# One seven-product step per unit turned into a mixed step, and another step's weight sum moved to the DMA, in a fused attention block

## The chip, the cores and the metric

The kernel runs on one core of a Trainium2 chip. The metric is the time on the device, in microseconds (us), of one execution; the median of three timed runs before the change is 1746.84 us (1742.09, 1746.84 and 1747.45). One further execution was recorded by the hardware profiler; it took 1742.72 us, and its span from the first to the last instruction is 1741.0 us.

## The reference

The input x has 256 rows of 4096 numbers. With the depth set to 1 only the attention layer runs:

```python
xn = rms_norm(x, norm_attn)
q, k, v, g = split(xn @ w_in_attn, 4)          # (256, 4096) @ (4096, 16384)
o = stick_breaking_attention(q, k, v)          # 32 heads of 128
h = x + (o * silu(g)) @ w_out_attn             # (256, 4096) @ (4096, 4096)
out = rms_norm(h, final_norm)
```

In the attention, each weight is a sigmoid of the scaled score times the product of one minus the sigmoids of the scores between it and the query, computed in log space, over strictly earlier positions.

Everything is float32. The two matrix products hold nearly all of the arithmetic.

## The kernel before, in words

**Exact products from three matmuls.** A float32 operand f is split into a rounded high part h (ScalarE casts it, `wh` for weights, `sh`/`oh` for the activations) and a low part l = f - h (VectorE subtracts, `wl`, `sl`/`ol`). A product is hh + hl + lh: three matmuls of 128x128 by 128x512 into one PSUM bank (`mm3`). So each weight tile costs one cast of ScalarE and one subtraction of VectorE before TensorE can use it.

**Units and steps.** The work is cut into 20 units. Units 0 to 15 belong to the input projection: unit u computes 256 columns of each of q, k, v and gate for all 256 rows. Units 16 to 19 belong to the output projection. A unit runs over the 4096 rows of its weights in 8 steps of 512 rows. A step has four raw weight tiles, named by (t, k): column half t, row half k, each 128x1024 numbers. They are loaded by SyncE into a ring of 8 buffers (`RAW_BUFS`), so two steps' tiles are held at a time; `load` (L427) issues them in a fixed order, and for steps with sums it takes the tile (1, 0) 2.5 places earlier.

**Saving products.** Units 0 and 16 are plain: 16 products per step. In all others a step seen as a 2x2 block product is of one of three kinds:

- a *full seven-product step* (`SEVEN_PARTS`, L97): a Strassen-like scheme. Seven weight parts, each of two 128x512 pieces, one product each: 14 products. Three of the seven parts are sums of raw tiles, beside a fourth that the load itself makes.
- an *eight-product step* (`EIGHT_PARTS`, L106): four parts, each used for two products per piece: 16 products, no sums of weights.
- a *mixed step* (`MIXED_PARTS`, L112): one of the two 128-row pieces goes by seven products, the other by eight: 15 products in six parts, the last with one piece only. Its sums are of 512 numbers per partition in place of 1024.

`SEVEN_IN` and `MIX_IN` list which steps of the input units are of the first and third kind, `SEVEN_AFTER` and `MIX_AFTER` those of the output units. Before, an input unit after the first has steps 1, 3, 4, 6 full, steps 0, 2, 5 mixed and step 7 eight-product: 4 x 14 + 3 x 15 + 16 = 117 products.

**The sums of weights.** For each full or mixed step:

- One sum (T3 in the code, `add_block`, L467) is made while loading: GpSimd issues a DMA that adds the block from memory onto the tile (1, 0): 512 KB for a full step, 256 KB for a mixed one.
- `sums` (L496) makes three more on VectorE: the difference for part 4, and the sums for parts 5 and 6 (for a mixed step: half as long, and the second of them is folded into part 4's tile).
- For the full steps listed in `FOURTH_IN` (input) the last sum, for part 6, is not made by VectorE but by a DMA that adds one SBUF buffer onto another (`moved_third`, L525), again issued by GpSimd, 512 KB. For these steps the difference is also due earlier (`FOURTH_AHEAD`, 6 us before its first product, against `SUMS_AHEAD`, 3 us).

Parts 5 and 6 of a step are used late: after the second part of the next step (L337 to L349). A step's tile is given back to the ring when its last subtraction and sum are done.

**Buffers.** There are 6 buffers for high parts (`PAIRS`) and 6 for low parts (`LOWS`), each of one part; ScalarE and VectorE can be at most six parts ahead of TensorE. The *lead* of a part is the time from the end of its low part on VectorE to its first matmul.

**The accumulators.** Seven PSUM banks hold the products of the scheme; at a unit's end `combine` (L805) adds them up on ScalarE and VectorE into `qk_sb` and `gv_sb`. The next unit's first products need those banks free. The eighth bank serves the attention of the two heads of the last unit (`head`, L929), whose small matmuls are put among the products of the following unit; its element work runs on ScalarE and VectorE.

**The order.** The class `Plan` (L139) runs a list schedule while the program is built: each engine has a clock, costs are formulas (`vector_ns`, `scalar_ns`, `tensor_ns`), and when an engine comes free the waiting operation with the earliest due time is emitted. Due times come from the place of a part's first product in the order of TensorE. The order of instructions on each engine is fixed by this; a change of the steps' kinds makes the whole order anew.

**The forms of x.** For each of 32 pieces of 128 rows of x (two per step) the forms for seven (7 forms) or eight products (6 forms) are made during unit 0 (`blocks_of`, `sums_of`); `SEVEN` (L88) has both pieces of a full step and the first of a mixed one.

The tables behind the counts above:

```python
SEVEN_PARTS = (
    part(0, 0, (1, "A11")), part(0, 1, (2, "A12")), part(1, 1, (3, "S4")),
    part(1, 0, (7, "S3")), part(0, 0, (6, "S2")), part(1, 1, (5, "S1")), part(0, 1, (4, "A22")),
)
MIXED_PARTS = (
    ((0, 0), 2, ((2, "A11", 1, 1), (4, "A21", 1, 1), (1, "A11", 0, 0))),
    ((0, 1), 2, ((2, "A12", 0, 0), (2, "A12", 1, 1), (4, "A22", 1, 1))),
    ((1, 1), 2, ((5, "A22", 1, 1), (3, "D2", 1, 1), (3, "S4", 0, 0))),
    ((1, 0), 2, ((5, "A21", 1, 1), (3, "D1", 1, 1), (7, "S3", 0, 0))),
    ((0, 0), 2, ((6, "S2", 0, 0), (4, "A22", 0, 1))),
    ((1, 1), 1, ((5, "S1", 0, 0),)),
)
```

Of the kernel before, what the change touches and what calls it, by code (L numbers as in the profile page):

```python
# [40 lines left out]

SEVEN_IN, MIX_IN = (1, 3, 4, 6), (0, 2, 5)
SEVEN_AFTER, MIX_AFTER = (1, 3, 6), (0, 2, 5)
RAW_BUFS = 8
PAIRS, LOWS = 6, 6
# [7 lines left out]
AHEAD, SUMS_AHEAD = 1.0, 3.0  # L55
PIPE = 1
T3_LEAD = 1500
FOURTH_IN, FOURTH_OUT = (1, 3), ()
FOURTH_AHEAD = 6.0
RAW_LEAD = 0  # L60
EARLY = 2.5
# [1382 lines left out]
```

## Time and profile before

| what | value |
|---|---|
| median of 3 timed runs | 1746.84 us |
| the profiled execution | 1742.72 us, span 1741.0 us |
| TensorE matmuls busy | 1713.9 us (98%) |
| TensorE weight loads busy | 1407.4 us (81%) |
| VectorE busy | 1630.2 us (94%) |
| ScalarE busy | 1227.0 us (70%) |
| GpSimd busy | 209.1 us (12%) |
| DMA | 434.84 MB, mean 250 GB/s |
| granted TensorE clock | 0.996 |

In the profile's rows PE is TensorE's matmuls, PEld its weight loads, DVE VectorE, ACT ScalarE, POOL GpSimd, and SP SyncE. A row of the order in time has the start in us from the span's start, the duration, the engine, the operation with out<-in, its shape, how many were merged (x), and in brackets the idle time before it and what ended it. A row of waits has who waited for whom, the total in us, how often, and the longest. All instructions show one line of the code (L158), since every one is issued through one helper of `Plan`, so rows are told apart by the names of tiles: `raw` raw weights, `wh` and `wl` their high and low parts, `acc` the PSUM banks, `sh`/`sl` forms of x, `oh`/`ol` forms of the attention's output.

### The profile page before, as it was taken

To read this page: it belongs to the slowest core of one execution; us is meant where nothing else is said; L and a number is where in the kernel's file an instruction comes from. 1 tells how busy PE (TensorE), PEld (TensorE's weight loads), DVE (VectorE), ACT (ScalarE), POOL (GpSimd) and SP (SyncE) were. 2 spreads that over 40 slices of the span, in tenths; PEclk is the share of its full clock that TensorE was granted. 3 is DMA by queue.
4 is the path that set the end of the run, shared out by engine and by line. 5 is a ranking of instruction groups with operands and counts; after the bars stand their busy time and mean duration, and the time that the engine had idled before them with its cause. 6 is when DMAs were issued, how large, how long until landed. Compare 5 with 4: busy or idle time off the path is not lost.

```text
span 1741.0 us, 23954 instructions
## 1 busy us (share of the span) xinstructions
PE 1713.9 (98%) x7690; PEld 1407.4 (81%) x7690; DVE 1630.2 (94%) x1872; ACT 1227.0 (70%) x1599; POOL 209.1 (12%) x224
## 2 busy tenths in 40 slices
PE   9999999999999999999999999999999999999997
PEld 6888888888888888888787878787888778888885
DVE  7889999999999999999999999999999987899997
ACT  7876777676777676767686767676767665666664
POOL 0010111011101011111111111111111022011100
PEclk9999999999999999999999999999999999999998
DMA  9998989888989898988888988889898778798886
GB/s 302 316 251 242 254 243 241 239 252 254 243 253 248 249 239 254 238 252 236 250 242 246 237 250 232 247 235 260 232 258 236 254 251 241 232 290 243 261 255 230
DMA packets 240543, 434.84 MB, mean 250 GB/s; under 512 B 25472, under 2 KB 45440, under 8 KB 240416
## 3 DMA queue, kind: packets, MB, share of 16 engines
q1 hardware_dynamic: 197616, 354.24, 62.0%
q0 software_dynamic: 41504, 77.22, 24.4%
q10 hardware_dynamic: 1296, 1.85, 0.3%
q8 instruction: 60, 0.98, 0.2%
q14 instruction: 67, 0.55, 0.1%
HBM read 407.52 MB, written 9.96 MB: 240 GB/s over the span
## 4 chain that ended last, share of the span: by engine, by line
PE 65%; DVE 13%; DMA 11%; issue 5%; ACT 4%; SPq 1%; POOL 0%; ACTq 0%; DVEq 0%; POOLq 0%
PE acc L158 62%; DMA raw<-in_w_in_dram 8%; DVE wl L158 8%; ACT wh L158 3%; DVE raw L158 3%; PE z L158 2%; DMA xres<-in_x_dram 1%; PE o L158 1%; SPq L158 1%; DMA p<-spill 1%; PE tr L158 1%; DMA raw<-in_w_out_dram 1%; ACT f L158 0%; DVE qk_sb L158 0%; DVE h L158 0%
## 5 line engine op out<-in xcount | busy, mean ns | idle before, releaser
L158 ACT CAST wh<-raw 128x1024 fp32r<-128x1024 f32 (+1 forms) x959 | 941.9, 1021 | 393.1 <-DMA raw<-in_w_in_dram 201.2
L158 DVE TENSOR_TENSOR wl<-raw,wh 128x1024 fp32r<-128x1024 f32 (+1 forms) x959 | 1100.8, 1184 | 60.3 <-ACT wh L158 57.0
L158 PE MATMUL acc<-wh,sh 128*128 128x512 f32 x1883 | 751.6, 399 | 4.3 <-DVE qk_sb L158 2.5
L158 PE MATMUL acc<-wl,sh 128*128 128x512 f32 x1883 | 735.9, 391 | 6.7 <-DVE wl L158 6.0
L158 PE MATMUL acc<-wh,sl 128*128 128x512 f32 x1883 | 735.6, 391 | 0.0
L158 PEld LDWEIGHTS acc<-wl,sh 128*128 128x128 f32 x1883 | 354.5, 188 | 85.2 <-DVE wl L158 15.7
L158 PEld LDWEIGHTS acc<-wh,sh 128*128 128x128 f32 x1883 | 354.2, 188 | 77.0 <-DVE qk_sb L158 5.8
L158 PEld LDWEIGHTS acc<-wh,sl 128*128 128x128 f32 x1883 | 353.8, 188 | 75.5 <-DVE sl L158 0.2
L158 DVE TENSOR_TENSOR raw<-raw,raw 128x1024 f32<-128x1024 f32 (+1 forms) x339 | 326.2, 964 | 2.0
L158 POOL DMA_DIRECT2D raw<-in_w_in_dram x105 | 127.9, 1218 | 931.6 <-DMA raw<-in_w_in_dram 522.9
L158 PE MATMUL acc<-wl,oh 128*128 128x512 f32 x485 | 189.5, 391 | 2.2 <-DVE wl L158 2.1
L158 PE MATMUL acc<-wh,oh 128*128 128x512 f32 x485 | 189.9, 391 | 0.0
L158 PE MATMUL acc<-wh,ol 128*128 128x512 f32 x485 | 188.8, 389 | 0.0
L158 PEld LDWEIGHTS acc<-wl,oh 128*128 128x128 f32 x485 | 91.1, 188 | 23.2 <-DVE wl L158 4.8
L158 PEld LDWEIGHTS acc<-wh,ol 128*128 128x128 f32 x485 | 91.1, 188 | 18.8
L158 PEld LDWEIGHTS acc<-wh,oh 128*128 128x128 f32 x485 | 91.1, 188 | 18.7
L158 ACT ACTIVATE f<-f 128x384 f32<-128x384 f32 x96 | 50.5, 526 | 3.0
L158 POOL DMA_DIRECT2D raw<-raw x30 | 26.5, 882 | 208.9 <-ACT f L158 86.7
L158 ACT CAST oh<-p 128x512 fp32r<-128x512 f32 (+3 forms) x41 | 19.3, 488 | 32.5 <-DVE p L158 16.6
L158 POOL DMA_DIRECT2D raw<-in_w_out_dram x18 | 21.5, 1192 | 136.2 <-DMA raw<-in_w_out_dram 105.4
L158 DVE SCALAR_TENSOR_TENSOR gv_sb<-acc,rin_v,gv_sb 128x512 f32<-128x512 f32 x45 | 33.5, 745 | 0.7
L158 POOL DMA_DIRECT2D p<-spill x41 | 22.9, 567 | 90.4 <-DVE ol L158 84.7
(88 smaller groups left out, 749.3 us busy)
## 6 DMA issues: line engine op xcount, KB each, us to landing
raw<-in_w_in_dram SPq DMA_DIRECT2D x1016, 256.0 KB, 5.0
raw<-in_w_out_dram SPq DMA_DIRECT2D x256, 256.0 KB, 5.1
raw<-in_w_in_dram POOLq DMA_DIRECT2D x60, 512.0 KB, 8.7
raw<-raw POOLq DMA_DIRECT2D x30, 512.0 KB, 6.8
raw<-in_w_in_dram POOLq DMA_DIRECT2D x45, 256.0 KB, 6.3
p<-spill POOLq DMA_DIRECT2D x41, 128.0 KB, 4.7
raw<-in_w_out_dram POOLq DMA_DIRECT2D x9, 512.0 KB, 8.8
xr<-in_x_dram SPq DMA_DIRECT2D x16, 256.0 KB, 5.5
```

The lines of the kernel that those rows point to most:

```text
L158: return self.tc.keep_in_program_order(getattr(self.engine, name)(*args, **kw))
```

## The change

In the fifteen input units after the first, step 3 becomes a mixed step in place of a full seven-product one, so the full steps are 1, 4 and 6 and the mixed ones 0, 2, 3 and 5. The step whose last sum a DMA makes is now step 4 alone, in place of steps 1 and 3. The change's own words also name "weights of the first product loaded first"; the diff has no line for that. Output units keep their steps.

```diff
-SEVEN_IN, MIX_IN = (1, 3, 4, 6), (0, 2, 5)
+SEVEN_IN, MIX_IN = (1, 4, 6), (0, 2, 3, 5)
 SEVEN_AFTER, MIX_AFTER = (1, 3, 6), (0, 2, 5)
...
-FOURTH_IN, FOURTH_OUT = (1, 3), ()
+FOURTH_IN, FOURTH_OUT = (4,), ()
 FOURTH_AHEAD = 6.0
```

## The prediction

> **What bounds the kernel now.** I read the page first, then the stretch in which the changed code runs by itself, then the matmuls in order of time, then the waits of that stretch, and last VectorE beside TensorE where the matmuls stop. The page, and the row of the stretch from the first product of the second projection unit to the first product of the output stage:
>
> ```profile
> PE 1713.9 (98%) x7690; PEld 1407.4 (81%) x7690; DVE 1630.2 (94%) x1872; ACT 1227.0 (70%) x1599; POOL 209.1 (12%) x224
> ...
> 97.70:1388.20 1290.50, 1282.15 (x5807) 1056.18 (x5806) 1237.85 (x1324) 929.96 (x1161) 161.17 (x154) 1.00 0.88 245
> ```
>
> In the second row the engines come in the order PE, PEld, DVE, ACT, POOL; then the granted clock (1.00), the share of the DMA engines (0.88) and GB/s. This stretch holds the fifteen units whose steps the change redistributes. TensorE is busy 99% of it and VectorE 96%. Two engines so close together do not say which one sets the time, so the matmuls have to be read one by one:
>
> ```profile
> 97.72 0.39 PE L158 MATMUL acc<-wh,sh 128*128 128x512 f32 x1
> ...
> 182.66 0.39 PE L158 MATMUL acc<-wh,sh 128*128 128x512 f32 x1
> ...
> 709.38 0.39 PE L158 MATMUL acc<-wh,sh 128*128 128x512 f32 x1
> 709.61 0.39 PE L158 MATMUL acc<-wl,sh 128*128 128x512 f32 x1
> 709.84 0.39 PE L158 MATMUL acc<-wh,sl 128*128 128x512 f32 x1
> 710.06 0.39 PE L158 MATMUL acc<-wh,sh 128*128 128x512 f32 x1
> ...
> 1388.17 0.39 PE L158 MATMUL acc<-wh,oh 128*128 128x512 f32 x1
> ```
>
> The first column is the start. A matmul lasts 0.39 us, but the next starts 0.227 us later; a product (three matmuls) takes 710.06 - 709.38 = 0.68 us. The rows at 97.72, 182.66 and 1388.17 are the first products of unit 1, of unit 2 and of the output stage. Unit 1 takes 84.94 us, and all fifteen take 1290.45 us, 86.03 us each. All run the same 117 products and two heads, so the mean unit loses 1.09 us to something that unit 1 does not meet: 16.4 us over the fifteen. That is nearly all that can be won in this stretch while TensorE does the same work. Who takes it is in the waits of the same stretch:
>
> ```profile
> ACT wh L158 <- DMA raw<-in_w_in_dram: 198.0, 130, 4.7
> ...
> DVE wl L158 <- ACT wh L158: 41.8, 58, 1.8
> ...
> PEld acc L158 <- DVE wl L158: 13.7, 20, 1.1
> ...
> PEld acc L158 <- DVE qk_sb L158: 5.8, 9, 1.1
> ```
>
> The columns are the total wait in us, its count and the longest. Only the last two rows hold TensorE: a weight load waits for VectorE's low part of the weights 20 times, and for an eviction of an accumulator 9 times, 19.5 us together. Loads run a little ahead of the matmuls, so the loss of the matmuls is smaller; following every start in these units, I find 15.1 us lost, and all of it in two places: 10.6 us in step 6 (first in unit 3, worst in unit 15) and 4.4 us at the first products of step 0 (units 2 to 14). Worst place, TensorE and then VectorE in step 6 of unit 15:
>
> ```profile
> 1370.38 0.40 PE L158 MATMUL acc<-wh,sh 128*128 128x512 f32 x1
> 1371.37 0.50 PE L158 MATMUL acc<-wl,sh 128*128 128x512 f32 x1 [0.60 <-DVE wl L158]
> ...
> 1372.63 0.40 PE L158 MATMUL acc<-wh,sh 128*128 128x512 f32 x1
> 1373.64 0.50 PE L158 MATMUL acc<-wl,sh 128*128 128x512 f32 x1 [0.61 <-DVE wl L158]
> ...
> 1374.90 0.39 PE L158 MATMUL acc<-wh,sh 128*128 128x512 f32 x1
> 1375.98 0.50 PE L158 MATMUL acc<-wl,sh 128*128 128x512 f32 x1 [0.69 <-DVE wl L158]
> ```
>
> ```profile
> 1364.95 1.83 DVE L158 TENSOR_TENSOR wl<-raw,wh 128x1024 fp32r<-128x1024 f32 x2 [0.81 <-ACT wh L158]
> 1366.69 1.22 DVE L158 TENSOR_TENSOR raw<-raw,raw 128x1024 f32<-128x1024 f32 x1
> 1367.83 1.22 DVE L158 TENSOR_TENSOR wl<-raw,wh 128x1024 fp32r<-128x1024 f32 x1
> 1368.96 1.22 DVE L158 TENSOR_TENSOR raw<-raw,raw 128x1024 f32<-128x1024 f32 x1
> 1370.10 1.22 DVE L158 TENSOR_TENSOR wl<-raw,wh 128x1024 fp32r<-128x1024 f32 x1
> 1371.23 1.22 DVE L158 TENSOR_TENSOR raw<-raw,raw 128x1024 f32<-128x1024 f32 x1
> ```
>
> Three times a gap of about 1.0 us stands in place of 0.227 us, 2.4 us in all. VectorE has no idle time from 1365 us on: it alternates low parts and sums of weights, each starting 1.135 us after the last. So the bound is TensorE's count of products, except at the end of step 6, where VectorE has run out of its lead, and at the unit's start, where an eviction stands behind other VectorE work.
>
> **The change, part by part.** Step 3 of each of the fifteen units goes from a seven-product step to a mixed one; step 1 loses its DMA-made sum and step 4 gets one.
>
> *TensorE.* A full step has seven parts of two products, 14; a mixed one has 3+3+3+3+2+1 = 15. One more product per unit, on the path that sets the end: 15 x 0.68 = +10.2 us.
>
> *VectorE.* Its two lengths and their spacing are in the rows above and in the first three here, from the start of unit 12 (the fourth, TensorE at the start of unit 2, is for the part on step 0):
>
> ```profile
> 1039.15 0.68 DVE L158 TENSOR_TENSOR raw<-raw,raw 128x512 f32<-128x512 f32 x1
> 1039.75 1.22 DVE L158 TENSOR_TENSOR wl<-raw,wh 128x1024 fp32r<-128x1024 f32 x1
> 1040.88 0.75 DVE L158 SCALAR_TENSOR_TENSOR qk_sb<-acc,rin_v,qk_sb 128x512 f32<-128x512 f32 x1
> ...
> 184.14 0.50 PE L158 MATMUL acc<-wh,sh 128*128 128x512 f32 x1 [0.63 <-DVE qk_sb L158]
> ```
>
> A 512-wide operation takes 0.60 us before the next starts. Step 3 has now seven low parts and two sums (its third is a DMA), 9 x 1.135 = 10.2 us against 14 x 0.68 = 9.5 us of TensorE. As a mixed step it has five long low parts, a short one and three short sums: 5 x 1.135 + 4 x 0.60 = 8.1 us against 10.2 us. Step 1 gets its third sum back, +1.135 us; step 4 gives one to the DMA, -1.135 us. In sum 2.1 us less per unit, and with TensorE's extra 0.68 us VectorE reaches the end of step 6 some 2.8 us earlier than now against the matmuls. That is over the 2.4 us that unit 15 loses there, and more than any other unit loses. I take 10.0 of the 10.6 us as recovered. The bounds: nothing, if VectorE waits there for weights instead of working (its wait of 0.81 us for ScalarE at 1364.95 is of that kind), and all 10.6 us.
>
> *Step 0.* The evictions that hold the first products (the operation on qk_sb at 1040.88) stand in the order of due times that the plan worked out, behind a sum and a low part. A VectorE that is ahead issues them sooner, but the order is made anew and need not favour them, since unit 1, which lost nothing in step 6, is followed by one of the longest of these waits (0.63 us at 184.14, the start of unit 2). Bounds 0 and 4.4 us; I take the middle, -2.2 us.
>
> *Step 1's sum on VectorE.* It is due 3 us before the product that uses it, which falls behind the second part of step 2. The place where VectorE's lead is thinnest is just ahead of that; VectorE and then TensorE, unit 13:
>
> ```profile
> 1144.15 1.22 DVE L158 TENSOR_TENSOR wl<-raw,wh 128x1024 fp32r<-128x1024 f32 x1
> 1145.40 0.69 DVE L158 TENSOR_TENSOR raw<-raw,raw 128x512 f32<-128x512 f32 x1
> 1146.01 2.35 DVE L158 TENSOR_TENSOR wl<-raw,wh 128x1024 fp32r<-128x1024 f32 x2
> ...
> 1146.85 0.39 PE L158 MATMUL acc<-wh,sh 128*128 128x512 f32 x1
> ```
>
> The low part that ends at 1145.4 is that of step 2's first part, used at 1146.85: 1.5 us of lead, the least among the units. Even if the sum went ahead of it, 0.3 us would be left, and by its due time it goes two low parts later, where the lead is 2 us and more. Bounds 0 and a stall of one sum, 1.135 us x 15 = 17 us; I take +1.0 us, nearest to the row's own lead. Behind the sum on VectorE stand the low parts of steps 1 and 2, and behind these their products.
>
> *Transfers.* The queue and the issues that are touched, and last the engines in unit 0:
>
> ```profile
> q0 software_dynamic: 41504, 77.22, 24.4%
> ...
> raw<-in_w_in_dram POOLq DMA_DIRECT2D x60, 512.0 KB, 8.7
> raw<-raw POOLq DMA_DIRECT2D x30, 512.0 KB, 6.8
> raw<-in_w_in_dram POOLq DMA_DIRECT2D x45, 256.0 KB, 6.3
> ...
> 0.00:97.70 97.70, 93.75 (x394) 74.47 (x395) 78.30 (x146) 80.36 (x152) 3.65 (x10) 0.98 0.94 309
> ```
>
> Fifteen of the thirty sums between buffers go (step 4's replaces one of two), and fifteen of the sixty 512 KB adding loads become 256 KB: 15 x (0.52 + 0.26) = 11.8 MB, by this queue's own rate (0.244 x 1741 us for 77.22 MB) 65 us of the sixteen engines, so their share falls by some 3 points. No row shows TensorE waiting for a DMA, so it counts as nothing directly; it helps the 198 us that ScalarE waits for weights. Step 4's sum takes 6.8 us beside loads for steps 5 and 6; now step 3's does the same for 4 and 5, without a loss of products there. POOL issues 15 instructions fewer. ScalarE loses 15 x 1.5 casts and has 30% to spare. In unit 0 one half-step's forms of x shrink from seven to six, under a VectorE that is busy for only 78.30 of that unit's 97.70 us (last row). Nothing in the diff alters the order of loads, though the words of the change speak of it: priced at nothing.
>
> *Sum.* +10.2 - 10.0 - 2.2 + 1.0 = -1.0 us. The profiled execution took 1742.72 us, which gives 1741.7 us. The timed runs are 1742.09, 1746.84 and 1747.45 us; with the profiled one, two executions near 1742.4 and two near 1747.1, whose middle is 1744.8 us. I predict 1744.8 - 1.0 = 1743.8 us.
>
> **The rivals.**
>
> *The supply of weights, not VectorE, empties the lead in step 6* (slower). For: 130 waits of ScalarE for loads, and VectorE's wait for ScalarE at 1364.95, just ahead of the stall. If every load for steps 5 and 6 comes at the present pace, the 2.8 us turn into idle time of VectorE, the stalls stay, and the product is paid in full: 1742.7 + 10.2 = 1752.9 us. It decides if less than 0.7 us per unit of stall goes. Against: after 1365 us VectorE does not wait at all while the lead is used up, and buffers are released sooner and DMA has less to do.
>
> *All stalls go.* 1742.7 + 10.2 - 16.4 = 1736.5 us. For: units 1, 5 and 7 show that a unit can run without a stall. Against: the step 0 waits occur also where VectorE is not late.
>
> *Step 1's sum makes a new stall* at the start of step 2, if the plan puts it ahead of the low parts there and ScalarE's cast comes late as well: at 0.75 us per unit +11 us on the forecast's 1741.7, 1752.7 us. It decides from 0.3 us of further delay.
>
> *VectorE is the bound everywhere.* Then its 2.14 us per unit would come off the end: 1742.7 - 32.1 = 1710.6 us. Against it stands the spacing of 0.227 us in the rows from 709 us, which no VectorE work lengthens there. The Trainium skill, "Perfetto Trace Analysis", section "Identifying the Most-Contended Engine", ranks VectorE by occupancy and warns against matmul busy time, taking the busy share of weight loads instead; by it (VectorE 94%, weight loads 81%) VectorE would be the engine to relieve, and this is the time that would follow. The trace disagrees for this kernel: the spacing of the matmuls shows TensorE full wherever VectorE is not late.
>
> **How the numbers follow.** Forecast 0.54 (near 1739 to 1748); all stalls go 0.17; supply-bound 0.16; new stall at step 1 0.11; VectorE-bound 0.02. The range takes the upper rivals to 1753 and the lower one to 1737; what lies beyond is some 0.15. A measurement here tells 0.3%, about 5 us, from no change. Faster by more: the rival without stalls and some of the forecast's lower edge, 0.25; slower: the supply and step 1 rivals, most of them, 0.21; the rest 0.54. The likeliest case's own range is 1739 to 1748 us.
>
> **What would show it.** Right: 15 more of each kind of matmul with sh; VectorE busy near 1598 us; long low parts 897 to 867 and sums between buffers by DMA 30 to 15; weight loads' wait for wl in the fifteen units down from 13.7 to under 3 us; the stretch from unit 1 to the output stage within 2 us of 1290.5. Wrong: the wait for wl stays at about 14 us (the supply rival), or moves to steps 1 and 2, or VectorE's idle time shrinks with the relief; the step 0 wait for qk_sb above 6 us would break that term alone.

## The result and the profile after

| | before | after |
|---|---|---|
| median of the timed runs of one session (7 each) | 1746.84 us | 1737.85 us |
| lowest to highest of these | 1741.97 to 1751.97 | 1736.91 to 1742.42 |
| ratio after / before | | 0.9957, 95% interval 0.9936 to 0.9978 |
| the profiled execution | 1742.72 us | 1738.73 us |
| VectorE busy | 1630.2 us | 1604.7 us |

The change made the kernel faster by 0.43%; the whole 95% interval lies below 1. The predicted 1743.8 us lies 6 us above the measured median; the case that came nearest is the rival in which all stalls go (1736.5 us). The medians differ by 9.0 us, the two profiled executions by 4.0 us only. What follows explains these 4.0 us; the other 5 us stand in no trace.

The page of the changed kernel, then its windows (in each row PE, PEld, DVE, ACT, POOL, granted clock, DMA share, GB/s): unit 0, the fifteen changed units, the output stage. Last, the first products of unit 1 and of the output stage in order of time:

```profile
PE 1716.8 (99%) x7735; PEld 1416.4 (82%) x7735; DVE 1604.7 (92%) x1868; ACT 1217.2 (70%) x1583; POOL 195.6 (11%) x209
...
0.00:98.10 98.10, 93.39 (x394) 73.16 (x395) 77.98 (x142) 80.47 (x151) 4.83 (x11) 1.00 0.93 308
98.10:1385.20 1287.10, 1286.02 (x5852) 1066.44 (x5851) 1212.25 (x1324) 920.11 (x1146) 146.48 (x138) 1.00 0.83 237
1385.20:1737.00 351.80, 337.36 (x1492) 276.84 (x1490) 314.44 (x405) 216.60 (x287) 44.29 (x60) 0.99 0.81 251
...
98.11 0.39 PE L158 MATMUL acc<-wh,sh 128*128 128x512 f32 x1
...
1385.18 0.39 PE L158 MATMUL acc<-wh,oh 128*128 128x512 f32 x1
```

The fifteen units took 1290.45 us before and take 1385.18 - 98.11 = 1287.07 us now, 3.4 us less with fifteen products more. Unit 0 is 0.4 us longer and the output stage 1.0 us shorter. So nearly the whole difference of the two profiled executions (4.0 us) lies where the steps changed. A stretch without any loss would last 15 x 84.94 = 1274.1 us at 117 products (the period of unit 1 before), and 10.2 us more, 1284.3 us, at 118 (0.68 us a product). The loss above that went from 16.4 us to 2.8 us.

The groups that show that the change did what it says, and the waits in the same stretch (total us, count, longest); the last row is that of before:

```profile
L158 DVE TENSOR_TENSOR wl<-raw,wh 128x1024 fp32r<-128x1024 f32 x867 | 1030.8, 1220 | 78.4 <-ACT wh L158 75.1 <-DMA raw<-in_w_in_dram 0.5
L158 PE MATMUL acc<-wh,sh 128*128 128x512 f32 x1898 | 755.6, 398 | 1.5 <-ACT wh L158 1.5
L158 DVE TENSOR_TENSOR raw<-raw,raw 128x1024 f32<-128x1024 f32 x147 | 179.5, 1221 | 1.5
L158 POOL DMA_DIRECT2D raw<-raw x15 | 13.2, 879 | 56.9 <-DVE wl L158 39.2 <-DMA raw<-in_w_in_dram 17.7
...
ACT wh L158 <- PE acc L158: 132.2, 190, 2.2
ACT wh L158 <- DMA raw<-in_w_in_dram: 114.7, 78, 4.2
...
PEld acc L158 <- DVE wl L158: 0.6, 1, 0.6
...
PEld acc L158 <- DVE qk_sb L158: 0.2, 1, 0.2
...
ACT wh L158 <- PE acc L158: 61.7, 75, 3.7
```

Fifteen more products (1898 against 1883), thirty fewer long low parts (867 against 897), fifteen DMA-made sums in place of thirty. The weight loads' wait for low parts fell from 13.7 us to 0.6 us and that for evictions from 5.8 us to 0.2 us. ScalarE's waits turned round: before, it waited 198.0 us for loads and, in the same stretch, 61.7 us (75 times) for TensorE to give its buffers back; now it waits 114.7 us for loads and 132.2 us (190 times) for TensorE. With six buffers of high parts, a wait of the casts for TensorE means that they are as far ahead as they may be.

### The profile page after: what moved, and what is told of

It reads as the page before. It is cut to its first block, busy times and chain, and to the rows that moved or that the text cites. A ratio compares the mean times of both kernels' runs of the same rounds, so it can differ in the third digit from the quotient of the medians.

```text
span 1737.0 us, 24005 instructions
## 1 busy us (share of the span) xinstructions
PE 1716.8 (99%) x7735; PEld 1416.4 (82%) x7735; DVE 1604.7 (92%) x1868; ACT 1217.2 (70%) x1583; POOL 195.6 (11%) x209
## 3 DMA queue, kind: packets, MB, share of 16 engines
q0 software_dynamic: 39344, 65.42, 20.9%
## 4 chain that ended last, share of the span: by engine, by line
PE 82%; DVE 7%; DMA 6%; ACT 2%; issue 2%; SPq 1%; POOL 0%; ACTq 0%; DVEq 0%
PE acc L158 78%; DMA raw<-in_w_in_dram 4%; DVE wl L158 4%; PE z L158 2%; DVE raw L158 1%; PE o L158 1%; DMA p<-spill 1%; ACT wh L158 1%; DMA raw<-in_w_out_dram 1%; PE tr L158 1%; SPq L158 1%; DVE gv_sb L158 1%; ACT f L158 0%; ACT gl L158 0%; DVE qk_sb L158 0%
## 5 line engine op out<-in xcount | busy, mean ns | idle before, releaser
L158 ACT CAST wh<-raw 128x1024 fp32r<-128x1024 f32 (+1 forms) x944 | 931.0, 1015 | 416.8 <-PE acc L158 174.2
L158 DVE TENSOR_TENSOR wl<-raw,wh 128x1024 fp32r<-128x1024 f32 (+1 forms) x944 | 1079.5, 1177 | 80.8 <-ACT wh L158 77.3
L158 DVE TENSOR_TENSOR raw<-raw,raw 128x512 f32<-128x512 f32 (+1 forms) x354 | 320.0, 908 | 2.7
L158 ACT ACTIVATE gl<-gl 128x512 f32<-128x512 f32 x48 | 30.1, 628 | 1.1 <-DVE gl L158 0.7
```

Source lines behind the costliest of these rows:

```text
L158: return self.tc.keep_in_program_order(getattr(self.engine, name)(*args, **kw))
```

## The experiments

The *stretch* below is always from the first product of unit 1 to that of the output stage in a kernel's profile, and the *loss* is what it has above 1274.1 us (117 products per unit), 1284.3 us (118) or 1294.5 us (119). *Room* is how much less VectorE work, or more TensorE time, a unit has than before, from the spacings of the prediction (1.135 us for a long operation, 0.60 us for a short one, 0.68 us for a product). Ratios are to the kernel before, run in the same session. Its median was 1746.91 us beside e1 to e4, 1741.88 us beside e5 to e8, 1746.23 us beside e9 to e11 and 1745.07 us beside e12, so medians of different sessions are not to be set side by side. Each stretch comes from one profiled execution, and the sessions ran on three chips, so small differences of stretches mean little. Stalls by step are found as in the prediction, by following the start of every matmul in a kernel's trace.

| kernel | products per unit | room, us per unit | stretch, us | loss, us | median, us | ratio (95% interval) |
|---|---|---|---|---|---|---|
| before | 117 | 0 | 1290.4 | 16.4 | | |
| after | 118 | +2.8 | 1287.1 | 2.8 | 1737.85 | 0.9957 (0.9936 to 0.9978) |
| e1 steps only | 118 | +2.8 | 1289.8 | 5.5 | 1742.32 | 0.9975 (0.9960 to 0.9989) |
| e2 sums only | 117 | -1.1 | 1300.6 | 26.5 | 1756.58 | 1.0050 (1.0031 to 1.0068) |
| e3 step 6's last parts later | 117 | 0 | 1298.2 | 24.1 | 1751.87 | 1.0039 (1.0018 to 1.0060) |
| e4 one sum left out | 117 | +1.1 | 1283.7 | 9.6 | 1734.13 | 0.9933 (0.9909 to 0.9957) |
| e5 sums of 1, 3, 4 by DMA | 117 | +1.1 | 1276.7 | 2.6 | 1729.13 | 0.9926 (0.9904 to 0.9948) |
| e6 earlier evictions | 117 | 0 | 1291.7 | 17.6 | 1742.58 | 1.0004 (0.9989 to 1.0019) |
| e7 step 6 mixed too | 119 | +6.8 | 1294.7 | 0.2 | 1745.71 | 1.0025 (1.0011 to 1.0040) |
| e8 after, sums of 1 and 4 by DMA | 118 | +4.0 | 1286.9 | 2.6 | 1738.10 | 0.9986 (0.9971 to 1.0002) |
| e9 before, sums of 1 and 4 by DMA | 117 | 0 | 1289.2 | 15.1 | 1742.26 | 0.9982 (0.9962 to 1.0002) |
| e10 after, no sum by DMA | 118 | +1.7 | 1286.2 | 1.9 | 1736.99 | 0.9958 (0.9944 to 0.9973) |
| e11 all four sums by DMA, step 6 late | 117 | +2.3 | 1302.9 | 28.8 | 1756.91 | 1.0064 (1.0043 to 1.0085) |
| e12 after, two low parts twice | 118 | +0.5 | 1314.8 | 30.4 | 1766.13 | 1.0121 (1.0095 to 1.0146) |

**The two halves of the change, each alone.** e1 has the new steps with step 1's sum by DMA; e2 has the old steps with step 4's sum by DMA.

```diff
e1, against after
-FOURTH_IN, FOURTH_OUT = (4,), ()
+FOURTH_IN, FOURTH_OUT = (1,), ()
e2, against before
-FOURTH_IN, FOURTH_OUT = (1, 3), ()
+FOURTH_IN, FOURTH_OUT = (4,), ()
```

> The changed steps (full 1, 4, 6; mixed 0, 2, 3, 5), but the DMA makes the last sum of step 1, not of step 4. Theory A (VectorE's lead runs out at the end of step 6, and the mixed step 3 gives it back): the mixed step alone brings 2.14 - 1.135 us plus... more exactly, against the changed kernel VectorE has the same load per unit, with 1.135 us less in step 1 and 1.135 us more in step 4, that is nearer to step 6. The lead at step 6 is then as in the changed kernel or a little less: stalls in step 6 under 3 us in all, profiled time 1737 to 1742 us. Theory B (the move of the sum to step 4 is what frees step 6): the step 6 stalls come back, 8 us and more, and the time is 1745 to 1753 us.

> The steps of before (117 products per unit), with the DMA making the sum of step 4 in place of those of steps 1 and 3. VectorE gets 1.135 us more per unit. Theory A: the lead at the end of step 6 falls by about 1.1 us in every unit, so the stall there grows by about 0.7 to 1.1 us per unit, 10 to 17 us in all: profiled time 1752 to 1760 us. Theory B (the place of the DMA's sum decides, not VectorE's load): faster than before, 1733 to 1740 us, as no product is added.

e1's stalls at products are 1.0 us in all, as theory A had it, and the profiled 1742.3 us is just above its upper end: 3.9 us are lost at the heads' matmuls instead, most of it where the scores wait for ScalarE's copy. e2 loses 10 us more than before, within theory A's 10 to 17 us, but not by theory A's path, so that hit is luck: step 6's stalls fell from 10.6 to 3.4 us, those at all products from 15 to 11.4 us, and 14.1 us are lost at the heads' matmuls, which lost nothing before. The waits of e2 in its stretch:

```profile
PEld o L158 <- ACT a L158: 10.1, 11, 1.6
PEld o L158 <- ACT gated L158: 8.1, 13, 0.7
PEld acc L158 <- DVE wl L158: 6.5, 12, 1.1
```

So the gain is the mixed step's; the move of the sums by itself, with one transfer fewer per unit, costs. Whether step 4's sum adds to the mixed step's gain is not resolved: e1's stretch is 2.7 us longer than the changed kernel's, but the intervals of the two ratios overlap.

**Relief without a product.** e4 leaves out one sum of weights in step 6 (the part goes in without its second addend), e5 lets the DMA make step 4's sum besides those of steps 1 and 3.

```diff
e4, against before, in third() of sums
+            if mixed or parts[a]["s"] != 6 or parts[a]["u"] >= OUT0:
                 yield add(near if mixed else (0, 1), (0, 1), e if mixed else g[0], place=1)
e5, against before
-FOURTH_IN, FOURTH_OUT = (1, 3), ()
+FOURTH_IN, FOURTH_OUT = (1, 3, 4), ()
```

> Before, with one sum of weights left out: the last one of step 6 in the fifteen units (its part then goes in without the second addend), so VectorE has 1.135 us less per unit just where TensorE stops; loads, casts, low parts and products stay. Theory A: the stalls in step 6 fall from 10.6 us to 1 to 4 us, and those of step 0 stay or fall a little: 1731 to 1738 us. Supply theory: stalls as before, 1741 to 1744 us profiled.

> Before (117 products per unit), with step 4's last sum made by the DMA as well, beside those of steps 1 and 3. VectorE is relieved by 1.135 us per unit, as in the kernel that left a sum of step 6 out, with no extra product and one more 512 KB adding transfer per unit. Theory A (VectorE's work per unit against TensorE's sets the loss, wherever in the unit the relief lies): stalls of the fifteen units from 15 to under 4 us, 1731 to 1736 us. Theory B (the supply of weights by the DMA is as tight): the third adding transfer delays the loads of steps 5 and 6, stalls stay at 10 us or more, 1740 us and over.

Both relieve VectorE by one long operation per unit, in different steps, and both are faster than before by some 0.7%. e4 loses nothing more in step 6 and 1.1 us at step 0; its remaining loss, 8.2 us, is at the heads' matmuls, where e5 loses nothing. Why the same relief leaves so different a rest is not shown. e5, with fifteen adding transfers more than before, has a stretch 10.4 us shorter than the changed kernel's, which is about the price of the fifteen products that it does not pay. The ratios do not tell these two apart, since their intervals overlap; but e8 below, the changed kernel with one more sum by DMA, ran in e5's session, with runs from 1735.25 to 1743.41 us against e5's 1726.88 to 1731.06 us. Queue q0 and the waits of e5's stretch:

```profile
q0 software_dynamic: 43664, 85.08, 27.5%
...
ACT wh L158 <- DMA raw<-in_w_in_dram: 143.8, 94, 5.6
...
PEld acc L158 <- DVE qk_sb L158: 1.4, 2, 1.2
PEld acc L158 <- DVE wl L158: 1.1, 2, 0.9
```

The adding queue is busier than before (27.5% against 24.4%), yet ScalarE waits less for loads (143.8 against 198.0 us), and TensorE hardly at all. This speaks against the supply rival: the transfers were not what held the kernel.

**The load of VectorE put back.** e12 is the changed kernel with two low parts of step 3 computed twice per unit, with the same result.

```diff
         yield dve(lambda: minus(l, full, h), (c.stop - c.start) * W, key_of(n, c))
+        if 0 < parts[n]["u"] < OUT0 and parts[n]["s"] == 3 and parts[n]["i"] in (1, 3):
+            yield dve(lambda: minus(l, full, h), (c.stop - c.start) * W, key_of(n, c))
```

> The changed kernel with two low parts of step 3 computed twice in each of the fifteen units, so that the second time writes the same numbers over the first: VectorE gets 2.27 us per unit back, about what the change took from it, while products, loads, sums and transfers stay as the change made them. VectorE then has 81.5 us of work in a unit of 85.6 us (before: 81.4 in 84.9). Load theory (the change gains because VectorE has less to do): stalls of 5 to 15 us return, 1743 to 1753 us. Supply theory (it gains by fewer and smaller adding transfers): no change, 1736 to 1740 us. Place theory (VectorE's load matters only where the unit's last steps stand): the extra work falls in step 3, where the mixed step leaves room, and costs under 3 us, 1738 to 1741 us.

The stretch grew by 27.7 us against the changed kernel's. The waits of e12 in it, its queue q0, the row of its stretch, and ScalarE, VectorE and TensorE in order of time in unit 2:

```profile
ACT wh L158 <- DMA raw<-in_w_in_dram: 185.4, 110, 7.9
ACT wh L158 <- PE acc L158: 58.8, 80, 3.7
PEld acc L158 <- DVE wl L158: 18.9, 24, 1.5
...
PEld acc L158 <- DVE qk_sb L158: 7.3, 12, 1.7
...
q0 software_dynamic: 39344, 65.42, 20.8%
...
98.50:1413.20 1314.70, 1299.39 (x5851) 1064.29 (x5850) 1235.19 (x1353) 913.34 (x1146) 146.30 (x138) 1.00 0.81 232
...
242.36 5.94 ACT L158 CAST wh<-raw 128x1024 fp32r<-128x1024 f32 x6 [7.92 <-DMA raw<-in_w_in_dram]
...
243.44 4.63 DVE L158 TENSOR_TENSOR wl<-raw,wh 128x1024 fp32r<-128x1024 f32 x4 [5.42 <-ACT wh L158]
...
243.46 0.51 PE L158 MATMUL acc<-wh,sh 128*128 128x512 f32 x1 [1.95 <-ACT wh L158]
```

These are much the waits of before, with the transfers of after: the adding queue moves the same 65.42 MB. ScalarE's wait for loads is back at 185.4 us, so VectorE's work alone can bring that wait about. The likely path is that VectorE gives the raw buffers back later; no row here shows this path by itself. The products lose nothing in steps 3 and 4, where the work was put, but 7.7 us in step 5, 11.2 in step 6 and 7.1 at step 0: the extra work is paid for later in the unit.

The size is more than any theory gave: 27.7 us for 15 x 2.27 = 34 us of work, though 0.5 us of room was left against before. So the load theory is borne out in its direction alone. VectorE was busy for about as long as before (1235.19 against 1237.85 us) and idle for longer (79.5 against 52.7 us), and yet the loss is 14 us larger. The rows of unit 2 show one such place: VectorE stands idle for 5.42 us behind a cast that waited 7.92 us for a load, and TensorE then waits as well. So there VectorE was not the engine that was full. The edit also lets the plan make the whole order anew and holds each of the two low parts back until it has been computed twice; which of these makes the excess is not settled.

**Order instead of load.** e6 gives the evictions an earlier due time; e3 uses step 6's last two parts behind the first part of step 7; e9 only changes which steps' sums the DMA makes.

```diff
e6, against before
-EVICT = 0
+EVICT = 3000
e3, against before
-                         late=at_ < last_seven)
+                         late=at_ < last_seven + (u < OUT0))
e9, against before
-FOURTH_IN, FOURTH_OUT = (1, 3), ()
+FOURTH_IN, FOURTH_OUT = (1, 4), ()
```

> Before, with the due times of all evictions at a unit's end 3 us earlier; no work added. If the 4.4 us at step 0 are a matter of order alone, they go and the time falls to 1737 to 1739 us. If VectorE simply has too much work per unit (theory A in its wider form), what the evictions gain the low parts of step 7 and step 0 or the sums lose: stalls change place, their sum stays within 4 us of 15, 1738 to 1747 us.

> Before, with the last two parts of step 6 of the fifteen units used behind the first part of step 7, as those of the other steps are; no work is added or moved between engines. Theory A: at the end of step 6 VectorE gets four products' time, 2.7 us, more for the same work, so the 10.6 us of stalls there go nearly all; the waits at step 0 may stay: 1730 to 1735 us. Supply theory (late weights, not VectorE's work, empty the lead): the same low parts come as late as now, and since every low part needs its weights in the same order the gain is under 4 us: 1738 us or more.

> Before (117 products), with the two DMA-made sums at steps 1 and 4 in place of 1 and 3: VectorE's load per unit is the same as before, only its place in the unit differs (1.135 us more in step 3, 1.135 us less in step 4). Load theory (VectorE's work per unit decides): stalls of the fifteen units 10 to 20 us, 1738 to 1748 us. Place theory (two full steps in a row, 3 and 4, whose transfers collide, made the trouble, so that one DMA sum less in step 3 and one more in step 4 cures it): stalls under 5 us, 1729 to 1734 us.

e6 moved the stalls: at step 0 they fell from 4.4 to 0.3 us, in step 6 they rose from 10.6 to 12.1 us, and 3.2 us came at the heads' matmuls; the ratio is 1.0004. e9 lost 15.1 us, like before. In both the plan made the order anew with VectorE's load unchanged, and the time stayed; so a lucky order is the less likely reason for the gains of the change, of e4 and of e5, though it is not excluded. e3 refutes theory A as I had put it there. The waits of e6, then of e3, in their stretches:

```profile
PEld acc L158 <- DVE wl L158: 17.0, 29, 1.1
```

```profile
PEld acc L158 <- DVE qk_sb L158: 11.4, 9, 1.9
PE acc L158 <- DVE qk_sb L158: 7.6, 8, 1.5
PEld acc L158 <- DVE wl L158: 5.7, 10, 1.1
```

In e3 the end of step 6 did lose its stalls (10.6 to 1.8 us), but those at step 0 grew from 4.4 to 12.2 us, now for evictions, and others came in step 4. So the shortage was not at one place only.

**The price of a product, and the rest of the change.** e7 makes step 6 mixed too; e8 and e10 vary the DMA-made sums of the changed kernel.

```diff
e7, against after
-SEVEN_IN, MIX_IN = (1, 4, 6), (0, 2, 3, 5)
+SEVEN_IN, MIX_IN = (1, 4), (0, 2, 3, 5, 6)
e8, against after
-FOURTH_IN, FOURTH_OUT = (4,), ()
+FOURTH_IN, FOURTH_OUT = (1, 4), ()
e10, against after
-FOURTH_IN, FOURTH_OUT = (4,), ()
+FOURTH_IN, FOURTH_OUT = (), ()
```

> The changed kernel with step 6 mixed too: 119 products per unit, and VectorE relieved by another 3.3 us per unit (ten long operations become five long and four short ones). In the changed kernel hardly a stall is left to win (0.5 us at products, about 2 us at the heads' matmuls), so the price of a product shows by itself: +10.2 us less at most 2.5 us, 1745 to 1750 us. If products were hidden behind VectorE (VectorE the bound everywhere), the time would fall or stay, 1730 to 1739 us.

> The changed kernel with step 1's last sum made by the DMA again, beside step 4's: VectorE relieved by 1.135 us more per unit. Theory A: nothing left to win but about 2 us at the heads, 1735 to 1740 us. If instead the removal of adding transfers was what the change gained by, it loses part of it: 1741 us or more.

> The changed kernel with no DMA-made sum at all: VectorE gets 1.135 us per unit back, POOL and the DMA lose fifteen adding transfers. VectorE then has about 80.4 us of work in a unit that TensorE needs 85.6 us for (before: 81.4 in 84.9; changed: 79.3 in 85.6). Load theory: between the two, stalls of 2 to 8 us in all, 1739 to 1746 us. If fewer adding transfers were what helped: 1734 us or less.

The stretch of e7 and its longest waits (no row of it has TensorE waiting):

```profile
99.10:1393.80 1294.70, 1294.70 (x5900) 1075.64 (x5899) 1179.90 (x1318) 910.50 (x1135) 148.78 (x143) 1.00 0.80 233
...
ACT wh L158 <- PE acc L158: 219.1, 284, 1.8
ACT wh L158 <- DMA raw<-in_w_in_dram: 39.2, 36, 3.6
```

TensorE is busy for the whole stretch, which is 7.6 us longer than the changed kernel's. The starts of its matmuls show no stall; those of the changed kernel show 0.5 us at products and 2.1 us at the heads' matmuls. With these 2.6 us that went away too, the fifteen products cost 10.2 us, as worked out. VectorE had 32 us less to do and the time rose. e8 and e10 lose 2.6 and 1.9 us in the stretch, beside the changed kernel's 2.8 us: with the mixed step in place it does not show there whether the DMA makes two sums, one or none. The ratio of e8 is weaker evidence: its interval includes no change, and its profiled execution is 3.4 us longer than the changed kernel's outside the stretch (453.3 against 449.9 us), for which I have no reason. For e10 I had expected stalls of 2 to 8 us; it lost 1.9 us in all, so 1.7 us of room suffice in this order.

**One step further.** e11 has all four sums by DMA and e3's order.

```diff
against before
-FOURTH_IN, FOURTH_OUT = (1, 3), ()
+FOURTH_IN, FOURTH_OUT = (1, 3, 4, 6), ()
-                         late=at_ < last_seven)
+                         late=at_ < last_seven + (u < OUT0))
```

> Before (117 products), with the last sums of all four full steps made by the DMA, and step 6's last two parts used behind the first part of step 7 so that its transfer has time. VectorE is relieved by 2.27 us per unit against before, by 1.135 us against the kernel with steps 1, 3 and 4. Load theory: little is left to win (about 2 us of stalls and 3 us of slightly stretched spacing), 1726 to 1731 us. If the fourth adding transfer of a unit is late, step 7's first parts wait for it or its evictions do: 1733 us or more.

It is slower than before, with 2.3 us of room. Its waits in the stretch and its queue q0:

```profile
PEld acc L158 <- DVE wl L158: 21.6, 44, 2.0
PEld tr L158 <- DVE gated L158: 4.9, 9, 1.0
...
q0 software_dynamic: 45824, 92.95, 29.7%
```

Low parts are late in every unit, in step 5 (7.3 us) and step 6 (5.8 us, most of it in unit 15), not at step 7 where I looked for it. Some 7 us more are lost at the heads' matmuls and 6 us at the products right behind them. Whether the fourth transfer or the later order does it wasn't tried apart; e3 shows that the order alone costs. With e12 it shows that the column of room does not put the losses in order: less work for VectorE is not enough by itself.

## Why the prediction was right or wrong

- **TensorE's product, +10.2 us: right.** e7 measured 10.2 us for the next such product.
- **Step 6, -10.0 us: right.** Its stalls went from 10.6 to 0.4 us. The reason was too narrow: a relief in step 4 removes these stalls as well (e5), more time at the end of step 6 only moves them (e3), and work added in step 3 brings them back (e12, by more than the work explains).
- **Step 0, -2.2 us: mis-sized.** The stalls went from 4.4 to 0.1 us, -4.3 us. I took them half for a matter of the order. e6 showed that the order only trades them against step 6's; with less work for VectorE both went together (e4, e5 and the change).
- **Step 1's sum, +1.0 us: not there.** No product of these units waits in step 1 or 2 of the changed kernel, and e10, with one more sum on VectorE, is as fast. What the changed kernel does lose anew is 2.1 us at the heads' matmuls, which the sum did not have.
- **Transfers, nothing directly: right.** e5 (more of them, and fast), e8 and e10 (fifteen more and fifteen fewer, with nearly the same loss) and e12 (the same, and slow) speak for it. The supply rival read ScalarE's 198 us wait for loads as a cause; e12 shows that it can be an effect.
- **The sum.** By these sizes it is +10.2 - 10.2 - 4.3 + 2.1 = -2.2 us; slightly closer spacing of the other matmuls gives another -1.0 us, unit 0 and the output stage -0.6 us together: -3.8 us, against 4.0 us measured between the profiled executions and -1.0 us forecast.
- **The base: the larger miss.** I put the forecast on the middle of four executions, 1744.8 us, and took for granted that the longer ones would stay. So 1743.8 us missed by 6 us, and 1737.85 us lies below the likeliest case's own range; it lies inside the whole range only because the rival without stalls had set the lower end, at 1737 us. The seven runs of before reach from 1741.97 to 1751.97 us, those after from 1736.91 to 1742.42 us: the medians differ by 9.0 us, the profiled executions by 4.0 us. Whether the longer executions of before hold more of the same stalls stays open, since only one was recorded. e5 and e10, with little loss, spread over 4.2 and 2.7 us, but so does e2, with much (4.1 us).
- **The signs.** The counts came out as said (15 more matmuls of each kind, 867 low parts, 15 sums by DMA), and the wait for low parts fell to 0.6 us. Two did not: VectorE was busy for 1604.7 us, not near 1598, and the stretch fell by 3.4 us, more than the 2 us allowed, by the sizes above. Why VectorE's busy time fell by 25.5 us in place of 32 is not settled.
- **VectorE the bound everywhere, 1710.6 us: wrong.** In e7 VectorE had still less to do and the time rose. In its stretch the weight loads are busy 1075.64 of 1294.70 us, 83%, with TensorE never idle. The Trainium skill, "Perfetto Trace Analysis", section "Identifying the Most-Contended Engine", takes this share, beside the rate of arithmetic, for the headroom of TensorE. The trace disagrees: in e7 83% is already full, so the 81% of the kernel before was nearly so.

## What to carry to other kernels

When two engines are both busy over 95%, look for the exact place where one holds the other and sum what is lost there. That sum (here 15 us of 1742) is about the most that a relief can bring in the recorded execution, and a relief paid for in the other engine's work has to be set against it. A stall at a thin place can be the shortage of a longer stretch showing itself; moving work or due times then moves the stall (e3, e6). Less work removed it (e4, e5, the change), but not in every order (e11). Before paying with work on the bounding engine, look for an engine with time to spare: a smaller relief of VectorE, paid by the DMA (e5), took 0.74% off the time, the change 0.43%. The intervals of these two ratios overlap; the stretches, 1276.7 against 1287.1 us, differ by the price of the fifteen products.

## What the runs showed that was not expected

- The price of VectorE's work is not a matter of its sum alone: 1.135 us per unit more than in the changed kernel had no price that shows (e10), while 2.27 us per unit more, 34 us in all, made the stretch 27.7 us longer (e12), although VectorE was then busy for about as long as before the change.
- The wait of an engine for loads can be the echo of a late consumer: 198.0 us before, 114.7 us after, 185.4 us in e12, with the transfers of e12 equal to those of after.
